# A decoder step of one layer: the search's counts shared between VectorE and ScalarE, rotary tables fetched at another time, more places for scores, and new costs in the planner

## The chip, the core and the metric

One core of a Trainium2 chip runs the whole step as one program. The metric is the device time in microseconds from launch to end; a profiled execution has besides it a span, from the first instruction to the last, which all views of the trace go by.

## The reference

One layer over 1024 prompt tokens and 64 sample tokens (8 requests of 8 tokens over a paged cache of 512), model width 1024. What matters here is the attention over selected keys:

```python
    dots = jnp.einsum('bthd,bld->bthl', qi.astype(jnp.float32), ki_all.astype(jnp.float32))
    score = jnp.einsum('bth,bthl->btl', wi.astype(jnp.float32), jax.nn.relu(dots)) * IDX_SCALE
    score = jnp.where(causal[None], score, -jnp.inf)
    _, idx = lax.top_k(score, n_sel)
```

Eight small indexer heads score every earlier token; the best 256 (130 for the samples) are kept, and the eight large heads attend over these alone. Around it stand a combined input projection with rotary turns of q, k and the indexer's q and k, a short convolution with gates, an output projection, a SwiGLU of width 2816, and a last gate with 256 extra features a token.

## The kernel before

**Tiling.** Activations are held feature by feature (128 partitions) times 1088 tokens, in chunks of 384, 384 and 320 tokens. Each fp32 factor is split in a high part (ScalarE copies it, rounded) and a low part (the rest, VectorE or GpSimd), and each product is three matmuls: high with high, high with low, low with high. So a projection of 128 features is 3 chunks of 24 matmuls each, and TensorE's total work is fixed by the shapes.

**The order of the work.** Nothing is scheduled by the compiler. A planner, the class Weaver, runs as the program is built. It has a clock for each engine, `T["pe"]`, `T["act"]`, `T["dve"]`, `T["pool"]`, and moves them with a cost for each operation (`act`, `tt`, `stt`, `ts`, `mm`, `mmf`, `mmg`, ...). Each stage is a generator that stops at `yield` for a buffer, an event or a moment; the planner goes on with the first side stream that is ready by these clocks, or else with the main stream, six matmuls at a time. The instructions come out in that order, and on the chip each engine runs its own in that order, waiting on semaphores. So a cost in the planner changes no instruction, only its neighbours. A side stream goes ahead if its data are there 0.2 us from TensorE's clock on and VectorE and ScalarE are planned no more than 5 us ahead (`LAG_E`, L292). A stream of the kind "dve" (the search) asks that VectorE's clock and its own time be within 1.5 us (L288).

```python
        self.go("act", 0.1 + n * 0.00084 + (1.3 if t != self.table else 0.0))
        c = max(0.426, n * 0.00168) if f32 else max(0.108, n * 0.000424)
        self.T["pe"] += max(0.108, n * 0.000424)
        self.T["pe"] += max(0.111, n * 0.000445 + 0.003)
```

These are the costs of a ScalarE operation (L127), of a side stream's matmul (`mm`, L181), of a projection's (`mmf`, L188) and of the second half's (`mmg`, L152).

**The stages.** Main: the indexer's k and q, then v, k, q, the convolution's gates, the branch gate ga; then, after everything else of the first half is done, output projection (two halves of 544 tokens), a projection of the extra features, gate-up by a seven-product scheme, down projection, last gate. Beside it as side streams, in this order of preference: `state_in`, `x_keep` (turns x to feature order and stores it in DRAM for the second half), `score_stream`, `samp_idx` (the samples' scores), `search` for the blocks 2 to 5 (group a) and for 6, 7 and the samples (group b), and at most three at a time of 32 `attn` streams (block, head pair) and 8 `samp_attn`. Attention starts when all scores are there (`ev_go`), and for blocks from 2 on when the block's threshold is known.

**Buffers.** Ring "p" has 5 places of 4 KB a partition: ki's high and low part hold two, `score_stream` two (query tiles, and `rbuf`, two places of 512 columns for rectified scores), so `x_keep` is left with one; later an attn stream takes two and a samp_attn three. Ring "L2" has 3: rotary tables take two, x_keep's turned tile one, later the convolution's rows. PSUM has three banks for projections ("pj"), two "at", two "pt", one "po". The planner doesn't know of the two places in `rbuf`; the chip's semaphores do.

**Rotary tables.** `load_tabs(64)` runs at the start, for the indexer's heads. `drop_tabs` (in `evac_qi`, last chunk of the last q block, and in `evac_q`) gives the two places back. The tables for k and q are fetched by `pre_tab(128)`, when the main stream comes to the first chunk of k.

**Scores and search.** For each head and each 512 columns `score_stream` does two matmuls into a bank "at", ScalarE rectifies into `rbuf`, and VectorE multiplies by the head's weight and adds to the scores (L139). `search` finds for each row the largest threshold that at least 256 scores reach, bit by bit of the float's 32: `cand` sets a bit, VectorE counts each block's scores from the threshold up (L1225, a compare with a summed output), `keep` compares the counts, `key` takes the bit. There are 33 rounds of counts: one for the sign, 31 bits, one last. What follows makes a bias of 0 or -2^100 for each score.

**Gate-up's start.** `norm` and four `factors` streams for each half p of the tokens make the sums and differences of the seven-product scheme (f_hi by ScalarE, f_lo by VectorE); weights go through the same treatment (`prep`, with `low` for the remainders). The first feature block runs on half 0, the second on half 0 and then 1.

## Time and profile before

| | |
|---|---|
| median of three runs | 1988.15 us (1983.81 to 1989.07) |
| the profiled execution: time, span | 1988.04 us, 1986.2 us |
| TensorE busy | 1942.3 us, 98% |
| VectorE, ScalarE, GpSimd busy | 1272.9 us (64%), 713.1 us (36%), 744.3 us (37%) |
| mean granted clock of TensorE | 0.989 of 2.4 GHz |

Times in rows are microseconds from the span's start unless marked ns. A line number is that of the helper that issues the operation, so groups are told apart by their tiles: pj, at, pt and po are PSUM banks, wh and wl (or whl) the parts of a weight tile, rt and ru the two halves of a rotary product, kidxT the samples' indexer keys, mx the row's maximum. Idle time of an engine is given with what ended it; where several semaphores were waited for, it is the last to come. A busy TensorE isn't one at full rate, so matmuls per stretch and the granted clock are read beside it.

### The profile page before, as it was taken

Reading aid. Unit: us, or ns where it says so; the run is one execution under the profiler, and the core shown is the slowest. Engines: PE = TensorE matmul, PEld = TensorE weight load, DVE = VectorE, ACT = ScalarE, POOL = GpSimd, SP = SyncE. Lnnn points to the kernel's source line nnn. Section 1 sums busy time; section 2 is a strip of 40 time slices with the busy share of each in tenths; the row PEclk is TensorE's granted clock in tenths of the full one; section 3 lists DMA queues with packets and bytes.
Section 4 is the critical chain, followed back from the end, with each engine's and each line's share of the span. In section 5 each row is a group of like instructions: output and inputs, shape, how many; then the busy total and the mean of one; then the engine's idle time right before and its main releaser. Section 6 shows DMA issues by size and latency. Waiting matters only on the chain.

```text
span 1986.2 us, 35764 instructions
## 1 busy us (share of the span) xinstructions
PE 1942.3 (98%) x13297; PEld 1863.8 (94%) x13297; DVE 1272.9 (64%) x2711; ACT 713.1 (36%) x1448; POOL 744.3 (37%) x661
## 2 busy tenths in 40 slices
PE   8998999999999999999999999999999999999998
PEld 5997879999999999879999999999999999999998
DVE  6534899899988896413437876566566653314754
ACT  5354433312433324433334532232232332213543
POOL 2533445323223233214454233232232364424883
PEclk9999999999999999999999999999999999999999
DMA  4574334222222222445443422222222353312343
GB/s 152 170 199 113 96 96 141 69 59 70 81 78 54 57 60 71 117 133 165 142 151 119 149 84 85 72 80 84 66 82 82 117 154 108 94 40 88 105 130 119
DMA packets 291240, 205.23 MB, mean 103 GB/s; under 512 B 28448, under 2 KB 270680, under 8 KB 291066
## 3 DMA queue, kind: packets, MB, share of 16 engines
q1 hardware_dynamic: 290742, 202.58, 34.4%
q8 instruction: 105, 1.72, 0.4%
q14 instruction: 69, 0.57, 0.1%
q10 hardware_dynamic: 324, 0.36, 0.1%
HBM read 151.43 MB, written 51.31 MB: 102 GB/s over the span
## 4 chain that ended last, share of the span: by engine, by line
PE 82%; DVE 4%; POOL 2%; issue 2%; DMA 1%; ACT 1%; SPq 0%; DVEq 0%; POOLq 0%; ACTq 0%
PE pj L154 44%; PE pj L190 27%; PE at L186 5%; PE po L186 4%; PE pt L197 3%; DVE scores L139 0%; DVE ru L135 0%; PE at L197 0%; POOL wl L150 0%; DVE junk L1225 0%; POOL rt L150 0%; POOL x L150 0%; DVE x L135 0%; DMA wraw<-in_w_down 0%; POOL x L2154 0%
## 5 line engine op out<-in xcount | busy, mean ns | idle before, releaser
L150 POOL TENSOR_TENSOR wl<-wraw,wh 128x512 fp32r<-128x512 f32 (+2 forms) x233 | 298.9, 1286 | 648.5 <-ACT wh L131 638.9
L190 PE MATMUL pj<-h_hi,wh 128*128 128x384 f32 (+2 forms) x1197 | 406.6, 340 | 0.3 <-ACT wh L131 0.3
L190 PE MATMUL pj<-h_hi,wl 128*128 128x384 f32 (+2 forms) x1197 | 393.7, 329 | 0.7 <-POOL wl L150 0.7
L190 PE MATMUL pj<-h_lo,wh 128*128 128x384 f32 (+2 forms) x1197 | 393.4, 329 | 0.0
L190 PEld LDWEIGHTS pj<-h_hi,wh 128*128 128x128 f32 (+1 forms) x1197 | 225.8, 189 | 16.4 <-issue 12.4
L131 ACT ACTIVATE wh<-wraw 128x512 fp32r<-128x512 f32 (+2 forms) x233 | 141.4, 610 | 277.5 <-PE pj L154 134.8
L190 PEld LDWEIGHTS pj<-h_lo,wh 128*128 128x128 f32 (+1 forms) x1197 | 226.1, 189 | 2.6
L190 PEld LDWEIGHTS pj<-h_hi,wl 128*128 128x128 f32 (+1 forms) x1197 | 225.5, 188 | 1.8 <-POOL wl L150 1.1
L154 PE MATMUL pj<-f_hi,whl 128*128 128x272 f32 x1056 | 208.3, 290 | 2.6 <-DVE whl L135 2.6
L154 PE MATMUL pj<-f_hi,wl 128*128 128x272 f32 x704 | 203.6, 289 | 0.5 <-DVE wl L135 0.5
L154 PE MATMUL pj<-f_hi,wh 128*128 128x272 f32 x704 | 203.4, 289 | 0.0
L154 PE MATMUL pj<-f_lo,wh 128*128 128x272 f32 x704 | 202.7, 288 | 0.0
L135 DVE TENSOR_TENSOR x<-pj,x 128x272 f32<-128x272 f32 (+2 forms) x144 | 67.0, 468 | 173.8 <-PE pj L154 170.6
L154 PE MATMUL pj<-m_hi,wh 128*128 128x272 f32 (+2 forms) x586 | 176.0, 300 | 0.9 <-ACT tha L131 0.5
L154 PE MATMUL pj<-m_hi,wl 128*128 128x272 f32 (+2 forms) x586 | 175.6, 300 | 0.0
L154 PE MATMUL pj<-m_lo,wh 128*128 128x272 f32 (+2 forms) x586 | 175.6, 300 | 0.0
L154 PEld LDWEIGHTS pj<-f_hi,whl 128*128 128x128 f32 x1056 | 170.5, 191 | 2.8 <-DVE whl L135 2.8
L154 PE MATMUL pj<-f_lo,whl 128*128 128x272 f32 x528 | 153.3, 290 | 0.0
L154 PEld LDWEIGHTS pj<-f_hi,wl 128*128 128x128 f32 x704 | 133.0, 189 | 0.8 <-DVE wl L135 0.8
L154 PEld LDWEIGHTS pj<-f_hi,wh 128*128 128x128 f32 x704 | 132.9, 189 | 0.0
L154 PEld LDWEIGHTS pj<-f_lo,wh 128*128 128x128 f32 x704 | 132.8, 189 | 0.0
L150 POOL TENSOR_TENSOR whl<-wraw,whl 128x512 fp32r<-128x512 f32 (+1 forms) x67 | 91.9, 1374 | 78.9 <-ACT whl L131 78.6
(367 smaller groups left out, 4534.1 us busy)
## 6 DMA issues: line engine op xcount, KB each, us to landing
wraw<-in_w_in SPq DMA_DIRECT2D x112, 256.0 KB
wraw<-in_w_gate_up SPq DMA_DIRECT2D x92, 256.0 KB
wraw<-in_w_down SPq DMA_DIRECT2D x40, 256.0 KB
wraw<-in_w_out SPq DMA_DIRECT2D x32, 256.0 KB
wraw<-in_w_ple_gate SPq DMA_DIRECT2D x32, 256.0 KB
x<-in_x_prompt SPq DMA_DIRECT2D x13, 512.0 KB
q_lo<-m_scr SPq DMA_DIRECT2D x19, 272.0 KB
m_scr<-q_lo SPq DMA_DIRECT2D x17, 272.0 KB
```

What stands on the lines that cost most here:

```text
L131: self.nc.scalar.activation(out, in_, func, **kw)
L135: self.nc.vector.tensor_tensor(out, a, b, op=op)
L150: self.nc.gpsimd.tensor_tensor(out, a, b, op=op)
L154: self.nc.tensor.matmul(ps, l, r, start=start, stop=stop)
L186: self.nc.tensor.matmul(ps, l, r, start=start, stop=stop)
L190: self.nc.tensor.matmul(ps, l, r, start=start, stop=stop)
L197: self.nc.tensor.transpose(ps, in_, ident)
```

## The change

The planner's costs of matmuls go from 0.424 to 0.45 ns a column and 1 ns (the second half's `mmg` is left as it is); the stream limits of 0.2 and 5 us become fields of a stream, and `norm` and `factors` of half 1 set theirs to 1.5 us. Ring "p" has 8 places; `rbuf` has four. The tables for k and q are fetched by a stream that starts where the indexer's tables are dropped, and the main stream waits for its event. In `search`, the blocks 4, 5, 6 and 7 are counted by ScalarE for the 31 bits: a sign of (threshold minus score) with summed output, which is the number below minus the number above. `keep` therefore compares with `lt` by "less or equal", and VectorE counts the other blocks from below. A score equal to the threshold counts half, so at the end the key's next larger value is tested once more with VectorE's exact counts and taken if it holds. The samples' attention is planned with longer times for page loads and GpSimd's scaling. No matmul is added or taken away.

```diff
-        c = max(0.426, n * 0.00168) if f32 else max(0.108, n * 0.000424)
+        c = max(0.426, n * 0.00172) / beside if f32 else max(0.11, n * 0.00045 + 0.001)
...
-        self.T["pe"] += max(0.108, n * 0.000424)
+        self.T["pe"] += max(0.11, n * 0.00045 + 0.001)
...
-                    ok = self._ready(s) <= pe + 0.2 and self.T["dve"] <= pe + LAG_E and self.T["act"] <= pe + LAG_E
+                    ok = self._ready(s) <= pe + s.ahead and self.T["dve"] <= pe + s.lag and self.T["act"] <= pe + s.lag
...
-    tp_ = tagged(tpool, "p", 5)
+    tp_ = tagged(tpool, "p", 8)
...
+    ev_tab = Ev()
+
+    def tabs_in(kind):
+        yield {"L2": 2}
+        load_tabs(kind)
+        ev_tab.t = W.move + 1.2
...
             if c == 2 and m == 3:
                 drop_tabs()
+                W.spawn(tabs_in(128))
...
-        rbuf = tp_([P, 2, 512], name="relu")
+        rbuf = [t[:, e] for t in (tp_([P, 2, 512], name="relu"), tp_([P, 2, 512], name="relu")) for e in range(2)]
...
-                    r = rbuf[:, used % 2]
+                    r = rbuf[used % 4]
...
+        def signs():
+
+            te, t0 = W.cur.t, W.cur.t
+            for i, q in enumerate(group):
+                if q in by_sign:
+                    m, L = lim(q)
+                    junk = tpool.tile([P, 1024], BF, tag="junk_s", name="junk_s", bufs=1)
+                    W.cur.t = t0
+                    W.go("act", 0.2)
+                    W.act(junk[:m, :L], score[q], AF.Sign, L, scale=-1.0, bias=cand[:m, i:i + 1].bitcast(F32),
+                          accum_out=cnt[:m, i:i + 1])
+                    te = max(te, W.cur.t)
+            W.cur.t = t0
+            return te
...
             W.stt(cand, key, 1 << b, msk, OP.bitwise_or, OP.bitwise_xor, G)
-            counts(OP.is_ge)
+            te = signs()
+            counts(OP.is_lt, on_dve)
+            W.cur.t = max(W.cur.t, te)
+            yield None
+            W.stt(keep, cnt, 1.0, lt, OP.mult, OP.is_le, G)
             W.stt(key, keep, b, key, OP.logical_shift_left, OP.bitwise_or, G)
             yield None
...
+        nc.vector.memset(cnt, 0.0)
+        counts(OP.is_ge, by_sign)
+        yield None
...
-        W.cur.t = t_k + 1.0
+        W.cur.t = t_k + 3.0
...
-        W.go("pool", 0.15 + LS * 0.00105)
+        W.go("pool", 0.15 + LS * 0.0029)
...
+        W.cur.lag = 5.0 if p == 0 else 1.5
...
-    sw = {64}
-
     def pre_tab(kind):
         def f(c):
-            if kind not in sw:
-                sw.add(kind)
-                yield {"L2": 2}
-                load_tabs(kind)
             if kind == 64:
                 yield ev_h[c]
                 if c == 0:
                     yield {"p": 2}
+            else:
+                yield ev_tab
         return f
...
-        W.spawn(search([2, 3, 4, 5], "a"), kind="dve", front=False)
-        W.spawn(search([6, 7, "s"], "b"), kind="dve", front=False)
+        W.spawn(search([2, 3, 4, 5], "a", (4, 5)), kind="dve", front=False)
+        W.spawn(search([6, 7, "s"], "b", (6, 7)), kind="dve", front=False)
```

## Rows read from the trace of the kernel before

**Rows 1.** The page's first part: busy time of each engine over the whole span, its share and its instructions.
```profile
PE 1942.3 (98%) x13297; PEld 1863.8 (94%) x13297; DVE 1272.9 (64%) x2711; ACT 713.1 (36%) x1448; POOL 744.3 (37%) x661
```

**Rows 2.** Windows of 50 us. Columns: the stretch and its length in us, then for each engine its busy us and (x) its instructions, the mean granted TensorE clock, the DMA engines' share and GB/s.
```profile
250.00:300.00 50.00, 46.81 (x250) 39.96 (x250) 46.06 (x88) 20.88 (x42) 23.36 (x20) 1.00 0.30 89
...
400.00:450.00 50.00, 50.00 (x304) 50.00 (x304) 46.58 (x123) 9.50 (x18) 11.14 (x12) 1.00 0.21 55
...
900.00:950.00 50.00, 50.00 (x304) 48.47 (x303) 16.71 (x24) 16.12 (x35) 20.15 (x17) 1.00 0.62 187
```

**Rows 3.** Windows of 10 us, with the same columns.
```profile
150.00:160.00 10.00, 6.95 (x25) 4.19 (x23) 3.47 (x7) 2.79 (x7) 3.01 (x3) 0.66 0.33 83
210.00:220.00 10.00, 10.00 (x48) 7.92 (x48) 8.07 (x22) 5.18 (x14) 3.29 (x3) 0.83 0.35 101
320.00:330.00 10.00, 7.28 (x34) 6.84 (x35) 9.53 (x26) 3.49 (x11) 8.13 (x12) 0.83 0.55 161
1130.00:1140.00 10.00, 7.27 (x41) 7.06 (x42) 9.90 (x17) 4.06 (x9) 4.24 (x3) 0.76 0.27 77
1140.00:1150.00 10.00, 10.00 (x74) 10.00 (x73) 9.16 (x17) 5.32 (x9) 3.00 (x2) 0.89 0.27 79
```

**Rows 4.** What TensorE waited for from 140 to 300 us: us in total, times, the longest.
```profile
PE at L186 <- ACT relu L131: 7.1, 4, 2.3
PE at L186 <- DVE kidxT L144: 4.0, 2, 3.1
```

**Rows 5.** The order of time from 138 to 162 us, VectorE and the SP queue (start, us, engine, line, operation, out<-in; in brackets the idle time before it and what the profile puts it down to), and the stores of x_keep in the whole run (ns: least, median, longest; first and last start).
```profile
143.37 0.64 SPq L163 DMA_DIRECT2D cos<-c_cos  x1
...
149.97 0.56 DVE L135 TENSOR_TENSOR rt<-pj,cos 128x384 f32<-128x384 f32 x1 [8.01 <-DMA out_new_v_prompt<-to]
...
L163 SPq DMA_DIRECT2D x_scr<-xT x9: 532/558/627, 79.2 to 207.6; - x9
```

**Rows 6.** The tile relu: the accumulation that reads it (ns: least, median, longest; first and last start), and what its engine waited for ahead of the instructions that touch it.
```profile
L139 DVE SCALAR_TENSOR_TENSOR scores<-relu,wi_c,scores x70: 341/750/1860, 106.7 to 301.3; 128x512 f32<-128x512 f32 x42, 128x384 f32<-128x384 f32 x14, 128x128 f32<-128x128 f32 x7, 128x256 f32<-128x256 f32 x7
...
  DVE scores L139: 23.3, 14
```

**Rows 7.** VectorE's groups by shape: the counts and the read of a count (busy us, mean ns), then when the counts of each of the two groups ran (first and last start).
```profile
L1225 DVE TENSOR_SCALAR_CACHE_REDUCE junk<-scores,candb 128x1024 uint8<-128x1024 f32 x33 | 42.2, 1279 | 1.2
...
L1225 DVE TENSOR_SCALAR_CACHE_REDUCE junk<-scores,candb 128x896 uint8<-128x896 f32 x33 | 37.8, 1146 | 1.2
...
L1225 DVE TENSOR_SCALAR_CACHE_REDUCE junk<-scores,canda 128x768 uint8<-128x768 f32 x33 | 33.4, 1012 | 1.2
L1225 DVE TENSOR_SCALAR_CACHE_REDUCE junk<-scores,canda 128x640 uint8<-128x640 f32 x33 | 29.0, 879 | 1.2
...
L1225 DVE DVE_READ_ACCUMULATOR junk<-scores,canda 128x1 f32 x132 | 10.9, 83 | 0.0
...
L1225 DVE TENSOR_SCALAR_CACHE_REDUCE junk<-scores,canda x132: 611/814/1016, 218.3 to 460.7; 128x384 uint8<-128x384 f32 x33, 128x512 uint8<-128x512 f32 x33, 128x640 uint8<-128x640 f32 x33, 128x768 uint8<-128x768 f32 x33
...
L1225 DVE TENSOR_SCALAR_CACHE_REDUCE junk<-scores,candb x66: 1145/1213/1281, 469.3 to 709.9; 128x896 uint8<-128x896 f32 x33, 128x1024 uint8<-128x1024 f32 x33
```

**Rows 8.** ScalarE's groups by shape: weight split, exponentials, the read of their sums, and the loads of function tables (busy us, mean ns, idle before).
```profile
L131 ACT ACTIVATE wh<-wraw 128x512 fp32r<-128x512 f32 x213 | 133.3, 628 | 193.4 <-PE pj L190 112.1 <-PE pj L154 58.3 <-issue 8.5
...
L131 ACT ACTIVATION_READ_ACCUMULATOR p<-p,mx 128x1 f32 x64 | 12.1, 188 | 0.0
...
L131 ACT ACTIVATE p<-p,mx 128x1024 f32<-128x1024 f32 x8 | 9.2, 1151 | 0.7 <-DVE mx L144 0.6
...
L131 ACT ACTIVATE p<-p,mx 128x896 f32<-128x896 f32 x8 | 8.3, 1039 | 4.4 <-DVE mx L144 4.4
...
L131 ACT ACTIVATE p<-p,mx 128x768 f32<-128x768 f32 x8 | 7.4, 930 | 2.2 <-DVE mx L144 2.2
...
L131 ACT ACTIVATE p<-p,mx 128x640 f32<-128x640 f32 x8 | 6.6, 822 | 0.8 <-DVE mx L144 0.8
...
L131 ACT ACT_TABLE_LOAD x4 | 5.1, 1283 | 3.2 <-issue 3.2
```

**Rows 9.** What TensorE waited for from 300 to 350 us (two of the lines).
```profile
PE pt L197 <- POOL p L1306: 1.5, 1, 1.5
PE po L186 <- DVE ptl L135: 1.5, 2, 1.2
```

**Rows 10.** What TensorE waited for from 720 to 1000 us (one of the lines).
```profile
PE pt L197 <- POOL psmp L1552: 1.5, 2, 1.2
```

**Rows 11.** What TensorE waited for from 1100 to 1160 us (one of the lines), and two of VectorE's instructions there.
```profile
PE pj L154 <- DVE whl L135: 2.6, 1, 2.6
...
1135.28 0.68 DVE L135 TENSOR_TENSOR whl<-wraw,whl 128x512 fp32r<-128x512 f32 x1
...
1150.96 0.43 DVE L135 TENSOR_TENSOR f_lo<-q_lo,f_hi 128x272 fp32r<-128x272 f32 x1
```

**Rows 12.** Windows over the searches, columns as in the second group.
```profile
301.00:461.00 160.00, 156.48 (x966) 154.90 (x965) 147.92 (x410) 44.67 (x105) 57.77 (x70) 0.99 0.33 90
461.00:712.00 251.00, 250.82 (x1614) 246.05 (x1613) 227.38 (x600) 87.06 (x185) 71.51 (x84) 1.00 0.24 65
```

**Rows 13.** ScalarE's groups from 360 to 740 us: exponentials and one tanh.
```profile
L131 ACT ACTIVATE p<-p,mx 128x384 f32<-128x384 f32 (+5 forms) x40 | 29.7, 743 | 13.3 <-DVE mx L144 13.1
...
L131 ACT ACTIVATE thb<-pj 128x384 f32<-128x384 f32 (+1 forms) x18 | 8.5, 474 | 42.0 <-PE pj L190 42.0
```

More of the change, by code (lines that the diff above doesn't have):

```diff
@@ L97, in __init__ @@
         self.front = self.queued = False
+        self.ahead, self.lag = 0.2, 5.0
 IDLE = "idle"
@@ L179, in later, with mm @@
         self.pending.append((self.cur.t, fn))
-    def mm(self, ps, l, r, n, start, stop, f32=False):
+    def mm(self, ps, l, r, n, start, stop, f32=False, beside=1):
         s = max(self.T["pe"], self.cur.t - 0.15)
-        c = max(0.426, n * 0.00168) if f32 else max(0.108, n * 0.000424)
+        c = max(0.426, n * 0.00172) / beside if f32 else max(0.11, n * 0.00045 + 0.001)
         self.T["pe"] = s + c
@@ L269, in run @@
         m = Stream(main)
-        LAG_D, LAG_E = 1.5, 5.0
+        LAG_D = 1.5
         while True:
@@ L1137, in score_stream @@
         tiles, seen, used = {}, [], 0
-        yield {"p": 2}
+        yield {"p": 3}
         qbuf = tp_([P, 2, 4, P], F32R, name="qstk")
-        rbuf = tp_([P, 2, 512], name="relu")
+        rbuf = [t[:, e] for t in (tp_([P, 2, 512], name="relu"), tp_([P, 2, 512], name="relu")) for e in range(2)]
         def fetch(w):
@@ L1197, in score_stream, with search, lim @@
                 W.cur.t = t0
-        W.give("p", 4)
+        W.give("p", 5)
         scores_done()
-    def search(group, nm):
+    def search(group, nm, by_sign):
         G = len(group)
+        def lim(q):
+            return (NS, LS) if q == "s" else (P, (q + 1) * P)
         for q in group:
@@ L1211, in search, with counts @@
         cnt = tpool.tile([P, G], F32, name=f"cnt{nm}")
+        lt = tpool.tile([P, G], F32, name=f"lt{nm}")
         for i, q in enumerate(group):
-            nc.vector.memset(N[:, i:i + 1], float(TOPK_S if q == "s" else TOPK))
+            n = float(TOPK_S if q == "s" else TOPK)
+            nc.vector.memset(N[:, i:i + 1], n)
+            nc.vector.memset(lt[:, i:i + 1], lim(q)[1] - 2 * n + 1 if q in by_sign else lim(q)[1] - n)
         nc.vector.memset(cand, 0)
         nc.vector.memset(cnt, 0.0)
-        def lim(q):
-            return (NS, LS) if q == "s" else (P, (q + 1) * P)
-        def counts(op):
+        def counts(op, which=None):
             for i, q in enumerate(group):
+                if which is not None and q not in which:
+                    continue
                 m, L = lim(q)
@@ L1226, in counts @@
                                         accum_out=cnt[:m, i:i + 1])
-            W.stt(keep, cnt, 1.0, N, OP.mult, OP.is_ge, G)
+        def signs():
[11 more added lines that the diff above has]
+            return te
+        on_dve = [q for q in group if q not in by_sign]
         counts(OP.is_ge)
+        W.stt(keep, cnt, 1.0, N, OP.mult, OP.is_ge, G)
         W.ts(key, keep, 31, None, OP.logical_shift_left, None, G)
@@ L1914, in norm @@
             room(p)
+        W.cur.lag = 5.0 if p == 0 else 1.5
         yield {"at": 2, "Q": 1}
```

18 lines of the change are left out of this document (added).

## The prediction

> **What bounds the kernel now.** I read the page's busy shares first: TensorE is busy for 1942.3 of 1986.2 us [rows 1]. The profiled execution took 1988.04 us, that is its span and 1.8 us around it, and agrees with the median of 1988.15, so sums made on the one hold for the other. In a kernel like this a busy engine off TensorE is worth nothing by itself; a change can only give back time in which TensorE stands still, or runs at its lower clock. So I looked next for that time. Where projections alone run, 50 us hold 304 matmuls [rows 2], 0.1645 us each for a mean of 362.7 columns (chunks of 384, 384 and 320); where search and projections run together (400 to 450 us) it holds 304 as well, with VectorE busy 46.58 of the 50 us. A VectorE at 93% thus costs TensorE nothing there. From 250 to 300 us it holds only 250. Then the 10 us windows with a low clock [rows 3]: at 150 to 160 the mean grant is 0.66, at 210 to 220 and 320 to 330 it is 0.83, at 1130 to 1140 0.76, at 1140 to 1150 0.89. Every one follows a wait of TensorE of over 2 us or two shorter ones close together, and since the lower level (1.2 GHz) is half of the upper (2.4 GHz), a mean of 0.66 over 10 us is 3.4 us lost on top of the wait. Then the waits themselves, stretch by stretch [rows 4, 9 to 11].
>
> The program is a list of instructions that a planner has put in order with its own cost for each. So I ask of each part: which wait goes, what the engine that is freed or loaded does then, and whether the planner's costs are as long as the rows.
>
> **Rotary tables early.** At 149.97 us VectorE starts the first rotary product of K after 8.01 us of idle [rows 5]. The bracket names an output transfer, the last of the queue to land before it; the tables it reads were issued just ahead, at 143.37 [rows 5]. The eight-column copy into kidxT that a TensorE matmul needs stands behind that product in VectorE's order, and TensorE waits for it: the longest of the two waits on kidxT is 3.1 us [rows 4], and the low clock after it costs 3.4 us [rows 3]. With the tables fetched when those of the indexer's rotary products are done, some 30 us sooner, both go: 6.5 us at most. The two issues move ahead of weight loads and of the reloads of x on SP's queue; if their places in L2 are not free, SP stands and later loads with it. The price is between nothing and the wait for a rope or two, of some three 0.56 us pieces each as at 149.97 [rows 5], 2 to 3 us, and the double-buffered weights cover it. x_keep is left with one L2 place instead of up to three; its stores ended at 207.6 us [rows 5] and nothing reads them before the second half, so a delay of tens of us is covered. I take 6.0 us of gain, ends 0 and 6.5.
>
> **Four places for rectified scores.** ScalarE's relu waits 23.3 us in 14 places for the VectorE accumulation that reads the place it wants [rows 6], and while it waits it doesn't empty PSUM: TensorE waits 7.1 us in four places, at most 2.3 us [rows 4]. The longest is the one ahead of the low clock at 210 us (1.7 us). Together 8.8 us. Two more places are worth two accumulations of 0.75 us [rows 6], 1.5 us of each wait. Of four waits of 1.8 us in the mean that takes 1.5 each, 6.0, and most likely the low clock, 1.7; against it, signs of about 1 us now stand in ScalarE's order between relus. I take 5.5 us, ends 0 and 8.8.
>
> **The counts on ScalarE.** VectorE loses, for each of 31 bits, the counts of 640 and 768 columns in the first group and of 896 and 1024 in the second: 0.879 + 1.012 + 1.146 + 1.279 us [rows 7] with 0.083 for each read, 4.65 us, 144 us in all. The exact last test puts back one such round (4.65 us) and some sixteen small operations on a few columns a group. ScalarE gains 31 rounds of four signs. No sign stands in the trace; the nearest rows are the exponentials with a pointer bias and an accumulated sum, 0.822, 0.930, 1.039 and 1.151 us and 0.188 for each read [rows 8]: 4.69 us a round, 145 us in all. So the work only changes engine. It was hidden: the two groups ran one after the other from 218 to 461 and from 469 to 712 us [rows 7], and TensorE lost almost nothing in 301 to 712 us but the few us of [rows 9] (156.48 of 160 and 250.82 of 251 us busy, [rows 12]). The searches will end sooner, perhaps by 100 to 200 us, attention follows sooner, and since projections are left to fill TensorE in any case, that is worth nothing in itself. What it can give is in places where attention waits for a loaded VectorE: the first heads wait 3.0 us between 300 and 350 us [rows 9] with 1.7 us of low clock; I take 2.0 of these 4.7 (from -2, if a sign stands ahead of an exponential). At the samples' attention, where the planner's waits for page loads and the pool's scaling are also made longer, the 1.5 us of waits on that scaling [rows 10] could go: I take 1.0, ends -1 and 1.5.
>
> **Gate-up's start.** The change lets the factors of the second half of the tokens be planned only while VectorE and ScalarE are less than 1.5 us ahead (5 before). The wait there, 2.6 us for whl [rows 11] with 2.4 and 1.1 us of low clock [rows 3], is a weight remainder that starts on VectorE only at 1135.28 because factors stand ahead of it. But VectorE is full there (9.90 and 9.16 of 10 us, [rows 3]) until the last remainder of those factors ends at 1151.4 [rows 11], and the first product with the second half needs them: if the weight comes sooner the factors come later, and TensorE waits a few us further on. I take 1.0, ends -3 and 6.1.
>
> **The planner's new costs.** A projection matmul was costed at 0.424 ns a column, 0.1538 us for 362.7 columns where 0.1645 is measured [rows 2]. The planner thus put 7% more TensorE work beside the other engines' work than it believed: a cushion. With 0.45 ns and 1 ns it has 0.1642, and the cushion is gone, while ScalarE's own costs stay short: a round of four signs is 4 x 0.2 + 4 x 0.1 + 3328 x 0.00084 = 4.00 us in its book and 4.69 by the rows, 0.69 x 31 = 21.4 us too little over the search. What queues behind a late sign is every relu, weight split and PSUM copy of ScalarE, and on VectorE, which stands at the keep operation until the signs have counted, every evacuation behind that. The planner has no slack against that but 1.5 us of lead for a search step, up to 5 us for the others, and the three projection banks of 24 matmuls (3.9 us each). New waits cost between 0 (ScalarE was busy 44.67 of 160 and 87.06 of 251 us [rows 12]; with 145 us of signs spread over 300 us it is at some 80%) and 27.4 us (below). I take 6.0, nearer to nothing, since in the DVE-bound stretch of [rows 2] work that was just as tight ended without loss, though it had the cushion.
>
> **Sum:** -6.0 - 5.5 - 2.0 - 1.0 - 1.0 + 6.0 = -9.5 us, on 1988.0: **1978.5 us**. The forecast's own range is 1966 to 1982.
>
> **Rivals.**
> *More comes off than that:* the upper ends of tables, places, heads, samples and gate-up (6.5 + 8.8 + 4.7 + 1.5 + 6.1 = 27.6 us) with 1 to 2 us of new waits: about 1962. For it: each of these waits has one cause, and the change names it. Against it: waits in a planned order mostly move. 0.08.
>
> *Nothing measurable:* new waits of 12 to 20 us on ScalarE's longer queue, each over 2 us with its 1.7 to 3.4 us of low clock, take back 15.5 us of gain: 1983 to 1994, middle 1988. For it: ScalarE's other work is costed short as well, such as the weight split of 512 columns, 0.628 us by the row [rows 8] and 0.53 in the planner's book. 0.20.
>
> *Slower, by ScalarE's drift:* place, 300 to 500 us, when both searches' signs run beside attention. ScalarE's deficit of 21.4 us and the lost cushion (7% of 200 us, 14 us) are 35.4 us; less some 8 us that lead and banks absorb, 27.4. With 15.5 gained: 2000 us. It decides from the point where ScalarE is planned nearly full, since a deficit drains in any gap: both groups' signs in turn, one pair of rounds each 5 to 6 us, would do that. 0.19.
>
> *Signs aren't in the loaded function table:* The trace has four table loads in all, of 1.283 us [rows 8], with relu, copy and exponential used side by side, and shows no sign. If each of the exponentials and tanhs beside the search (40 and 18 in 380 us [rows 13]) is switched to and back, that is 58 x 2 x 1.283 = 149 us of ScalarE time on 132 busy (at the rate of 87.06 in 251 us, [rows 12]) and 145 of signs: 426 us in a stretch of 380, and some 45 us are lost, 2033 us. The Trainium skill ("ScalarE: Activation LUTs", section "Table sets: the hidden batching unit") says that cheap functions, relu, copy, identity and abs, are in every set as filler, doesn't name sign among them, and prices a switch at 2.66 us, by which the same 116 switches would be 309 us. The trace agrees for relu and copy, which cause no load. 0.03.
>
> **How the numbers follow.** Forecast 0.50. About 0.3%, 6 us, is what a measurement of this kernel can tell from no change: faster is below 1982, slower above 1994. Forecast and first rival give faster 0.58, the second same 0.20, the last two slower 0.22. For 8 in 10 the range leaves out about 0.07 below and 0.11 above: 1962 to 1999.
>
> **What would show it.** Right: no 8 us idle of VectorE before the first rotary product of K, no wait on kidxT over 2 us, clock 1.00 at 150 to 160 us; relu's waits on the accumulation under 8 us; searches that overlap and end before 600 us; still four table loads. Gate-up's start should keep most of its loss, as a wait for factors or weights. Wrong: waits of TensorE on ScalarE or VectorE between 300 and 550 us over 10 us in sum, with clock below 0.95 there; or table loads by the dozen.

## The result and the profile after

The changed kernel takes 2014.25 us (2012.23 to 2019.87, four runs) where the kernel before, timed on the same chip, takes 1988.13: a ratio of 1.0143, 95% interval 1.0128 to 1.0158. It is slower by 26 us. The forecast was 1978.5 us, and the wider of its two ranges ended at 1999.

The page's first part and its row of the granted clock, after (the columns are those of [rows 1]; the clock in tenths, one digit for each fortieth of the span):
```profile
PE 1952.6 (97%) x13297; PEld 1867.2 (93%) x13297; DVE 1153.4 (57%) x2512; ACT 834.6 (41%) x1696; POOL 745.3 (37%) x661
...
PEclk9999989999999999999999989999999999999999
```
VectorE has lost 119.5 us of work and ScalarE has gained 121.5, as the change intends. TensorE has the same 13297 matmuls and takes 27.3 us more of span.

Where the time went is read from a count that needs no model: how many matmuls TensorE has done by a given time. Each number is the (x) of TensorE in a window that starts with the span.

| kernel | by 280 us | by 460 us | by 1100 us | by 1300 us |
|---|---|---|---|---|
| before | 1417 | 2487 | 6667 | 8207 |
| after | 1428 | 2363 | 6503 | 7992 |

At 280 us the changed kernel is 11 matmuls ahead. At 460 it is 124 behind; before does (2487 - 1417) / 180 = 5.94 a us there, so that is 21 us. At 1100 it is 164 behind, 25 us at the 6.53 a us of before from 460 to 1100, and at 1300 it is 215 behind, 28 us at 7.7 a us. (The mix of wide and narrow matmuls differs a little between kernels, so such a figure is good to a few us.) From 11 ahead to 215 behind is 226 matmuls: 135 are lost from 280 to 460 us, 40 from 460 to 1100, and 51, some 7 us, from 1100 to 1300, at gate-up's start. So most of the loss arises between 280 and 460 us.

Windows of after (columns of [rows 2]); the first two are stretches of [rows 3], the last is the stretch of the loss:
```profile
150.00:160.00 10.00, 10.00 (x61) 8.87 (x61) 4.57 (x9) 6.08 (x15) 1.77 (x2) 1.00 0.49 132
210.00:220.00 10.00, 9.06 (x48) 6.48 (x47) 9.71 (x19) 7.36 (x17) 3.95 (x4) 1.00 0.32 95
248.00:258.00 10.00, 9.08 (x32) 7.42 (x33) 6.74 (x17) 5.08 (x13) 1.90 (x3) 0.66 0.11 32
289.00:299.00 10.00, 7.60 (x36) 7.60 (x37) 7.53 (x29) 5.89 (x16) 2.73 (x3) 0.66 0.18 60
...
410.00:420.00 10.00, 6.27 (x24) 6.18 (x24) 8.81 (x26) 6.57 (x16) 4.03 (x4) 0.66 0.25 67
...
1170.00:1180.00 10.00, 3.66 (x13) 3.03 (x14) 8.58 (x18) 3.54 (x7) 0.40 (x1) 0.50 0.08 29
280.00:460.00 180.00, 158.73 (x937) 153.21 (x937) 158.33 (x481) 122.82 (x274) 72.89 (x91) 0.95 0.33 93
```
The two low clocks of [rows 3] at 150 and 210 us are gone (1.00, and 61 matmuls where 25 stood). New ones stand at 248, 289 and 410 us, at 0.66, and at 1170 us with 0.50: there TensorE ran the whole 10 us at the lower level. From 280 to 460 us it is busy for 158.73 of 180 us (before: 175.46, with clock 0.99). VectorE is busy for 158.33 there and ScalarE for 122.82: neither is full.

What TensorE waits for, after: first from 140 to 300 us (compare [rows 4]; the 5.3 us of mx are the same wait as in the second view), then from 280 to 460, then from 1120 to 1200 us (compare [rows 11]).
```profile
PE at L187 <- DVE mx L1352: 5.3, 1, 5.3
PE at L187 <- ACT relu L132: 4.4, 4, 2.2
PE at L187 <- ACT kidxT L132: 1.5, 1, 1.5
```
```profile
PE at L187 <- DVE mx L1352: 6.5, 2, 5.3
PE po L187 <- DVE ptl L136: 5.9, 4, 3.7
PE at L187 <- DMA qh<-qh_scr: 5.7, 4, 3.7
PE pt L198 <- POOL p L1364: 2.8, 3, 1.4
```
```profile
PE pj L155 <- DVE f_lo L136: 6.5, 3, 4.4
PE pj L155 <- ACT f_hi L132: 2.0, 1, 2.0
```
From 280 to 460 us it is mostly VectorE that TensorE waits for, in attention (the row maxima mx and the split ptl: 12.4 of 20.9 us). The next is the load of a head's queries, qh (5.7 us, 0.5 before); the longest of these loads was held for 3.7 us until VectorE's lob, the last step of group a's search, gave back a place of the same ring. ScalarE has no row there. At gate-up the wait for the weight remainder of [rows 11] is gone, and waits for the factors of the second half of the tokens stand in its place.

ScalarE's groups by shape, after: the signs with the idle time ahead of them, the read of their counts, the table loads. Under them the tile junk_s: what VectorE waited for from it (us, times).
```profile
L132 ACT ACTIVATE junk_s<-scores,candb 128x1024 bf16<-128x1024 f32 x31 | 35.6, 1150 | 1.0
L132 ACT ACTIVATE junk_s<-scores,candb 128x896 bf16<-128x896 f32 x31 | 32.2, 1039 | 19.3 <-DVE candb L140 19.0
L132 ACT ACTIVATE junk_s<-scores,canda 128x768 bf16<-128x768 f32 x31 | 29.0, 936 | 1.0
L132 ACT ACTIVATE junk_s<-scores,canda 128x640 bf16<-128x640 f32 x31 | 25.6, 826 | 41.9 <-DVE canda L140 41.9
...
L132 ACT ACTIVATION_READ_ACCUMULATOR junk_s<-scores,candb 128x1 f32 x62 | 11.6, 188 | 0.0
...
L132 ACT ACT_TABLE_LOAD x4 | 5.1, 1283 | 3.2 <-issue 3.2
```
```profile
  DVE keepb L140: 19.9, 16
  DVE keepa L140: 3.9, 7
```
The signs take what the exponentials of [rows 8] take, to 6 ns, and there are still four table loads. ScalarE stands idle for 41.9 and 19.0 us ahead of its signs until VectorE's candidate comes, and VectorE stands for 23.8 us until signs have counted (10.0 of them from 280 to 460 us): in a chain of rounds each waits for the other. That VectorE is the later one is read from what TensorE waits for, above, and from the lengths that follow.

VectorE's small steps of group a, after (four columns, mean ns), and one stretch in order of time, VectorE and GpSimd (columns of [rows 5]):
```profile
L140 DVE SCALAR_TENSOR_TENSOR keya<-keepa,keya 128x4 int32<-128x4 int32 x31 | 12.0, 388 | 1.1
L140 DVE SCALAR_TENSOR_TENSOR keepa<-cnta,lta 128x4 int32<-128x4 f32 x31 | 11.9, 382 | 4.1 <-ACT junk_s L132 3.9
L140 DVE SCALAR_TENSOR_TENSOR canda<-keya,mska 128x4 int32<-128x4 int32 x31 | 11.8, 381 | 0.8
```
```profile
298.36 0.17 DVE L140 SCALAR_TENSOR_TENSOR canda<-keya,mska 128x4 int32<-128x4 int32 x1
...
301.21 1.30 POOL L151 TENSOR_TENSOR wl<-wraw,wh 128x512 fp32r<-128x512 f32 x1 [3.33 <-ACT wh L132]
301.79 0.73 DVE L140 SCALAR_TENSOR_TENSOR keepa<-cnta,lta 128x4 int32<-128x4 f32 x1
302.46 1.01 POOL L151 TENSOR_TENSOR rt<-rt,ru 128x384 f32<-128x384 f32 x1
302.56 0.93 DVE L140 SCALAR_TENSOR_TENSOR keya<-keepa,keya 128x4 int32<-128x4 int32 x1
303.43 1.28 POOL L151 TENSOR_TENSOR wl<-wraw,wh 128x512 fp32r<-128x512 f32 x1
303.52 1.21 DVE L140 SCALAR_TENSOR_TENSOR canda<-keya,mska 128x4 int32<-128x4 int32 x1
304.69 1.41 POOL L1364 TENSOR_SCALAR p<-p,mx 128x128 f32<-128x128 f32 x4
```
The same step on four columns takes 0.17 us while GpSimd is idle and 1.21 us while GpSimd works. Read the ends: keepa ends at 302.52 and GpSimd's wl at 302.51; keya at 303.49 and rt at 303.47; canda at 304.73 and wl at 304.71. Three times a step of a few columns ends 10 to 20 ns after the GpSimd instruction that was running when it started. The planner books 0.134 us for each. These three are not picked out: of the 190 such steps of both searches in this trace, the 134 beside an idle GpSimd took 144 to 166 ns, and the 38 that took more than 250 ns all started beside a running GpSimd instruction and ended 7 to 27 ns after the end of one.

What stood ahead of the longest of TensorE's waits, the 5.3 us on mx (VectorE first, the last line is TensorE's):
```profile
280.14 1.24 DVE L140 SCALAR_TENSOR_TENSOR keepa<-cnta,lta 128x4 int32<-128x4 f32 x1
281.42 0.93 DVE L140 SCALAR_TENSOR_TENSOR keya<-keepa,keya 128x4 int32<-128x4 int32 x1
282.27 1.83 DVE L140 SCALAR_TENSOR_TENSOR scores<-relu,wi_c,scores 128x512 f32<-128x512 f32 x1
284.14 0.99 DVE L136 TENSOR_TENSOR scores<-scores,b 128x128 f32<-128x128 f32 x1
...
291.04 0.29 DVE L1352 CUSTOM_DVE_ANT_0 p<-at,b 128x128 f32<-128x128 f32 x1
291.40 0.47 PE L187 MATMUL at<-k_hi,qh 128*128 128x128 f32 x1 [5.26 <-DVE mx L1352]
```
The two small steps take 1.9 us more than they are booked for, the accumulation 1.2 (0.66 booked) and the addition 0.8 (0.23 booked); a little later VectorE stands 0.66 us until a sign has counted. So in this wait the small steps are the largest part, but not the only one.

### The profile page after: what moved, and what is told of

Read it like the earlier page. It is cut to its first block, busy times and chain, and to the rows that moved or that the text cites. A ratio compares the mean times of both kernels' runs of the same rounds, so it can differ in the third digit from the quotient of the medians.

```text
span 2013.5 us, 35917 instructions
## 1 busy us (share of the span) xinstructions
PE 1952.6 (97%) x13297; PEld 1867.2 (93%) x13297; DVE 1153.4 (57%) x2512; ACT 834.6 (41%) x1696; POOL 745.3 (37%) x661
## 4 chain that ended last, share of the span: by engine, by line
PE 72%; DVE 6%; issue 2%; ACT 2%; POOL 1%; DMA 1%; SPq 0%; DVEq 0%; POOLq 0%; ACTq 0%
PE pj L155 43%; PE pj L191 20%; PE po L187 4%; PE at L187 3%; PE pt L198 2%; DVE junk L1239 1%; ACT junk_s L132 1%; DVE cum L1319 0%; POOL wl L151 0%; DMA q<-ple_scr 0%; DVE q_lo L136 0%; DVE x L136 0%; POOL whl L151 0%; DVE f_lo L136 0%; DVE cv L140 0%
## 5 line engine op out<-in xcount | busy, mean ns | idle before, releaser
L151 POOL TENSOR_TENSOR rt<-rt,ru 128x384 fp32r<-128x384 f32 (+5 forms) x81 | 82.4, 1026 | 105.1 <-ACT ru L132 52.5
```

The source lines that it names most:

```text
L151: self.nc.gpsimd.tensor_tensor(out, a, b, op=op)
```

## The experiments

The theory at this point: VectorE is late against the planner's book between 200 and 520 us, because the book has its two-input operations too short, and the old, too short cost of a matmul had hidden that. The rivals: ScalarE's queue of signs is late (the forecast's own rival); the larger ring lets attention heads start into a loaded VectorE; the small steps are simply many. In the expectations theory A is the lost cushion of 7%, theory B the two searches beside attention on VectorE, theory C the larger ring. Ratios are to the kernel before on the same chip, with their 95% intervals. The runs are from several chips, on which the kernel before takes 1985.9 to 1988.4 us, so a difference between two runs' times is good to some 2 us.

**The old matmul costs in the changed kernel.**
```diff
-        c = max(0.426, n * 0.00172) / beside if f32 else max(0.11, n * 0.00045 + 0.001)
+        c = max(0.426, n * 0.00168) / beside if f32 else max(0.108, n * 0.000424)
...
-        self.T["pe"] += max(0.11, n * 0.00045 + 0.001)
+        self.T["pe"] += max(0.108, n * 0.000424)
```


> The changed kernel with the planner's old costs of a matmul (0.424 ns a column in mm and mmf), all else as changed. Theory A (the 7% cushion): most of the new waits between 280 and 460 us go, about 2014 - 17 = 1997 us. Theory B (the searches with signs run beside rotary products and attention on VectorE): the waits stay, 2006 us or more. Theory C (three attention streams at a time by the larger ring): as B.


1997.63 us, 1.0056 [1.0039, 1.0073]: 16.6 us come back from two cost lines that add no work and remove none, as theory A had it. By 1100 us 6620 matmuls are done (after: 6503).

**All counts on VectorE in the changed kernel**, the rest as it is:
```diff
-        W.spawn(search([2, 3, 4, 5], "a", (4, 5)), kind="dve", front=False)
+        W.spawn(search([2, 3, 4, 5], "a", ()), kind="dve", front=False)
```
and the same for group b.


> The changed kernel with every block counted by VectorE for the 31 bits, none by ScalarE (the last test then counts nothing), all else as changed. Theory B: the searches run one after the other again, attention of the blocks from 2 on starts after 450 us, and the waits between 280 and 460 us fall from 24 us to under 8: about 1996 us. Theory A: VectorE is as full as before and without the cushion, so 2008 us or more. Theory C: some waits go since attention comes later, 2002 to 2008 us.


1997.06 us, 1.0053 [1.0038, 1.0069]: 17.2 us come back here too. By its expectation that is theory B's result, and theory A's (2008 us or more) is missed: without the cushion, but with all counts on VectorE, this stretch loses nothing. Windows over the loss for these two kernels, in this order:
```profile
280.00:460.00 180.00, 165.68 (x984) 162.99 (x983) 154.43 (x455) 118.24 (x264) 71.36 (x83) 0.95 0.31 85
```
```profile
280.00:460.00 180.00, 178.17 (x1106) 176.64 (x1104) 171.74 (x473) 46.63 (x107) 70.01 (x81) 1.00 0.33 93
```
With VectorE *fuller* by 13 us (171.74 for 158.33), TensorE loses nothing in this stretch. So it isn't VectorE's load as such that hurts. One reading is that it is how far the book is from it: counts are booked as long as they are, small steps aren't, and with the counts on VectorE the 93 small steps of group a spread over 238 us (207.6 to 445.8) instead of 175, with 4 of group b's steps ahead of 460 us instead of 50. But the small steps still take 11.9 us more than booked between 280 and 460 us here (19.2 after, 12.8 before), without a cushion and without loss, so the distance to the book isn't the whole account: that attention meets one search there and not two is as good a reading of this run.

**The old lead of 5 us for gate-up's factors**, in the changed kernel:
```diff
-        W.cur.lag = 5.0 if p == 0 else 1.5
+        W.cur.lag = 5.0
```


> The changed kernel with the lag of norm and factors of the second half of the tokens at 5 us again. All theories of the first half: nothing moves ahead of 1000 us. If the lag is what makes TensorE wait for f_lo and f_hi at gate-up's start (8.5 us of waits and 6.8 us of low clock there): 5 to 8 us less than the changed kernel, about 2007 us, with the wait for a weight back in its place. If VectorE is simply too full there: within 2 us of 2014.


2008.52 us, 1.0098 [1.0071, 1.0126]: 5.7 us come back by the medians. The f_lo and f_hi waits go, and the wait for whl of [rows 11] returns. The 20 us after 1160 us, first after, then with this edit:
```profile
1160.00:1180.00 20.00, 11.48 (x74) 10.42 (x73) 17.98 (x39) 9.06 (x16) 1.68 (x2) 0.75 0.17 55
```
```profile
1160.00:1180.00 20.00, 18.24 (x144) 17.88 (x143) 17.64 (x32) 9.54 (x18) 5.64 (x4) 1.00 0.24 74
```

**A smaller ring**, in the changed kernel (6 places for p, one of them not given back to attention):
```diff
-    tp_ = tagged(tpool, "p", 8)
+    tp_ = tagged(tpool, "p", 6)
...
-        W.give("p", 5)
+        W.give("p", 4)
```


> The changed kernel with a ring p of 6 places of which one isn't given back after the scores, so that x_keep has one place and attention five (two streams at a time) as before the change; rectified scores keep their four places. Theory C: the waits of attention between 280 and 460 us fall by half, about 2002 us. Theories A and B: 2010 us or more.


2026.42 us, 1.019 [1.0162, 1.0219]: slower by another 12 us. The rival of the ring (theory C, 2002 us) falls; with fewer places the waits on VectorE are longer (ptl 10.7 us in nine places, where after has 6.2 in five).

**The parts alone, on the kernel before.** First the tables, the four places with the ring, and the samples' times together; then the new matmul costs alone; then the new search alone.


> The kernel before with the rotary tables early, the larger ring with four places for rectified scores, and the longer planned times in the samples' attention; matmul costs, lag and search as before the change. Each of costs and search, undone alone, took 17 us off the changed kernel. If the two add (two separate troubles): 2014 - 17 - 17 - 6 (lag) = 1974 us, some 13 us faster than before. If they are one trouble that needs both (VectorE late in a stretch without slack): undoing the second gains little more, 1985 to 1992 us.


1986.76 us, 1.0005 [0.9992, 1.0018]: no change. The parts do what they say: by 280 us 1481 matmuls are done, 64 more than before, some 11 us. By 460 us the lead is 32, by 1100 us 9. Half of it is given back from 280 to 460 us, to waits for ptl (4.4 us), mx (3.2) and GpSimd's p (2.6) that were 1.5, nothing and 1.5 before; most likely attention, coming earlier, meets more of the search on VectorE.

> The kernel before with the planner's new matmul costs alone. Theory A (the cushion): without it the loaded VectorE reaches TensorE also without signs, 1994 to 2002 us. If the cushion only counts beside the signs: within 4 us of 1987.


2006.93 us, 1.0098 [1.0076, 1.0121]: 19 us lost by telling the planner the truth about TensorE alone. About half is lost ahead of 280 us (1345 matmuls by then, 72 fewer than before, some 14 us), where TensorE waits 14.0 us on relu in eight places; by 1100 us 153 are missing. Ahead of 280 us it is above all the accumulations of scores that are booked too short.

> The kernel before with the new search alone (signs, last test, and the added stop between counting and keeping, by which the two searches run side by side). Theory B: attention meets both searches on VectorE, 1996 to 2004 us. If the signs only hurt without the cushion: within 4 us of 1987.


2002.16 us, 1.0079 [1.0057, 1.0101]: 16 us lost by the new search alone, with TensorE waiting for ptl (6.6 us) and mx (3.8).

**One search after the other**, in the kernel before with the new search: group b starts when a is done.
```diff
+        if nm == "b":
+            yield ev_first
...
+        if nm == "a":
+            ev_first.t = W.cur.t
```


> The kernel before with the new search alone (it took 16 us more than before), and the second group's search held until the first has its thresholds. If two searches side by side, with three small VectorE operations each a bit, crowd VectorE as attention runs: back to 1986 to 1991 us. If it is the signs in ScalarE's queue and VectorE's stand at keep: 1998 us or more.


1997.88 us, 1.0045 [1.0031, 1.0059]. Side by side costs at most some 4 us of the 16: the two intervals overlap, and the control below shows that a new order alone moves the time by 3. The rest comes with one search at a time as well. The expectation had put 1998 us down to the signs in ScalarE's queue and VectorE's stand at keep, so this run speaks for that rather than for two searches that crowd VectorE.

**Tables alone and places alone**, on the kernel before.


> The kernel before with the rotary tables for k and q fetched early, alone. As predicted before the change: 6 us less, 1980 us, with VectorE's 8 us idle at 145 us, the 3 us wait on kidxT and the low clock after it gone. If the wait only moves: within 2 us of 1986, with as much lost ahead of 300 us.


1989.49 us, 1.002 [1.0007, 1.0032].


> The kernel before with the ring p of 8 and four places for rectified scores, alone. As predicted: 5.5 us less, 1980.5 us, TensorE's 7 us of waits on relu down to 2 to 3 us. Rival: the late VectorE, no longer held back at relu, is met a little later by the first attention heads: the loss goes from ahead of 300 us to 300 to 350 us, and the time stays at 1986.


1988.78 us, 1.0026 [1.0013, 1.004]. Each removes the waits that it aims at and gains nothing: without VectorE's idle time ahead of K's rotary products, TensorE waits 7.0 us on relu in seven places and once 4.3 us on ptl; without the relu waits, 3.7 us on mx and 4.7 on kidxT.

**How much any other order moves the time.** In the kernel before, one cost of the planner is made 1 ns longer (VectorE's two-tensor operations).
```diff
-        self.go("dve", 0.1 + n * 0.00104)
+        self.go("dve", 0.101 + n * 0.00104)
```


> A control: the kernel before with 1 ns more on the planner's cost of each two-tensor operation of VectorE. Nothing is meant by it; the orders of the engines come out somewhat otherwise. It tells how far any new planning moves the time: within 2 us of 1986 if single effects of 3 to 5 us may be read as causes, 4 us or more off if they may not.


1992.92 us, 1.0017 [1.0003, 1.003]. A second one, 10 ns on ScalarE's operations, gave the like:


> A second control: the kernel before with 10 ns more on the planner's cost of each ScalarE operation. As the first control: within 2 us of 1986, or 4 us and more off it, if any new order moves the time that far.


1990.98 us, 1.0014 [1.0002, 1.0026]. So a new order as such can cost 3 us; the tables' and places' 1.002 and 1.0026 are hardly more. That an order can gain as much by luck wasn't seen, but two controls don't rule it out.

**VectorE's lengths in the planner's book**, in the changed kernel: 0.28 us more for each score accumulation, 1.0 us more for the small steps of each bit. No instruction is added. The 0.28 is what the trace shows in the mean (the 70 accumulations take 58.6 us where 39.9 are booked); the 1.0 is more than it shows (0.75 in group a, 0.24 in group b), and 0.7 of it stands at keep, where VectorE also waits for the signs.
```diff
+                    W.go("dve", 0.28)
...
+            W.go("dve", 0.3)
...
+            W.go("dve", 0.7)
```


> The changed kernel with the planner told how long VectorE's operations were measured to be in the score stretch: 0.28 us more for each accumulation of scores, and 1.0 us more for the three small operations of a bit (they took 0.39 to 0.55 us each beside scores, 0.13 planned). No instruction changes. If TensorE waits because VectorE's real queue is longer than the planned one: the waits between 280 and 460 us fall from 34 to about 18 us, near 1997 us. If the planned lengths don't matter: 2010 us or more.


1994.97 us, 1.0046 [1.0034, 1.0058]: 19.3 us come back. By 280 us 1482 matmuls are done, 54 more than after, and from 280 to 460 us 1052, 20 fewer than before instead of 135; by 1100 us 6669 are done, as before (6667). What is left stands at gate-up (8165 by 1300 us, before 8207: 5.5 us). The lead of 5 us on top of that:


> The changed kernel with the lag at 5 us again and the planner told of VectorE's measured lengths (as in the run that took 19 us off). If the two parts add: 1995 - 6 = 1989 us, and what stays over the kernel before is attention beside two searches. If they don't: 1993 us or more.


1988.35 us, 0.9996 [0.9985, 1.0008]. The two together take back the whole 26 us.

**The same book with the old search.** First with the old matmul costs (tables, places, samples' times, book), then with the new ones, which is all of the change but the search and gate-up's lead.


> Tables early, larger ring with four places, longer planned times of the samples' attention; search, lag and matmul costs as before the change; and the planner told of VectorE's measured lengths (0.28 us more for each accumulation of scores, 1.0 us more for the small operations of a bit). If VectorE's late queue is what the first attention heads meet: 8 to 12 us less than without these lengths, 1974 to 1979 us, faster than both kernels. If not: 1984 to 1988 us.


2034.9 us, 1.0249 [1.0231, 1.0267]. A miss: 49 us above the kernel before. With TensorE booked 7% too short and VectorE at its full length the plan most likely paces the search too slowly: group b's counts end at 777 us (712 before). TensorE waits 27.2 us on m_hi in four places ahead of the out-projection and once 11.1 us for a head's qh.


> As the one before, with the new matmul costs. With VectorE's lengths in the planner's book the cushion isn't needed: within 4 us of the one before, 1974 to 1982 us. If the cushion covers more than these operations: 1990 us or more.


1983.23 us, 0.9986 [0.9975, 0.9996]: between its two expectations, and the one version that beats the kernel before, by 0.14%, which is no more than the controls moved the time. From 280 to 460 us TensorE is busy for 179.53 of 180 us.

**Shorter GpSimd instructions**, to tell whether the small steps are long because of GpSimd. Two-input operations of 256 columns or more go in pieces of 128, with the planner's costs left alone.
```diff
+        if len(out.shape) == 2 and n >= 256:
+            for x in range(0, n, 128):
+                y = min(n, x + 128)
+                self.nc.gpsimd.tensor_tensor(out[:, x:y], a[:, x:y], b[:, x:y], op=op)
+            return
```


> The changed kernel with GpSimd's two-input multiplications and additions of 256 columns or more written as pieces of 128 columns each; the planner's costs, and so what it books, are left as they are. Theory V (VectorE runs late because its operations with two inputs in SBUF stand still until GpSimd's running operation has ended, so that a 4-column step of the search that takes 134 to 166 ns beside an idle GpSimd takes 600 to 1290 ns beside a busy one): the longest of these steps fall to some 400 ns, VectorE gains some 15 us between 200 and 520 us, and the time falls from 2014 to 1998 to 2006. Theory N (VectorE is late by the number of its operations alone, 62 pairs of steps more than before, and the long steps are waits for other things that the trace puts into their durations): the long steps stay long, and the time stays at 2010 or above, a little more by the added GpSimd instructions.


2028.41 us, 1.0214 [1.0194, 1.0235]. Theory V's time is missed; by its time alone the run would fall to theory N (2010 us or above, though by more than a little), but the long steps shorten, which N excludes. The trace says why. Group a's small steps in it, then GpSimd's largest group, after (512 columns) and here (128):
```profile
L140 DVE SCALAR_TENSOR_TENSOR keepa<-cnta,lta 128x4 int32<-128x4 f32 x31 | 10.8, 349 | 3.8 <-ACT junk_s L132 3.6
L140 DVE SCALAR_TENSOR_TENSOR keya<-keepa,keya 128x4 int32<-128x4 int32 x31 | 9.6, 310 | 1.1
...
L140 DVE SCALAR_TENSOR_TENSOR canda<-keya,mska 128x4 int32<-128x4 int32 x31 | 8.6, 276 | 0.8
```
```profile
L151 POOL TENSOR_TENSOR wl<-wraw,wh 128x512 fp32r<-128x512 f32 x213 | 283.6, 1334 | 596.1 <-ACT wh L132 570.7 <-PE pj L191 5.9 <-DVE mx L145 4.5
```
```profile
L154 POOL TENSOR_TENSOR wl<-wraw,wh 128x128 fp32r<-128x128 f32 x892 | 433.0, 518 | 559.5 <-ACT wh L132 546.3 <-DVE mx L145 4.1 <-DVE ptl L136 1.9
```
The small steps shorten (1151 to 935 ns for the three; canda's longest from 1289 to 494 ns, but keepa's grows from 1244 to 1802), VectorE's busy time over the span falls from 1153.4 to 1090.4 us, and by 1100 us 6599 matmuls are done, 96 more than after: 15 us, the gain that theory V expected by that time, of which the small steps' 31 x 0.216 = 6.7 us are a part. But four pieces take 2.07 us where one took 1.33, GpSimd's work grows from 745.3 to 1018.7 us, and late in the kernel, where TensorE waits on GpSimd's chain (x 8.5 us, longest 7.0), more than that is lost.


> The kernel before with the early tables, the four places and larger ring, the samples' times, the new matmul costs and VectorE's measured lengths in the planner's costs (1983.2 without this edit), and with GpSimd's two-input operations of 256 columns or more in pieces of 128. The old search stays. Theory V: its small steps between counts shorten in the same way, and since the planner books them at their long lengths here, the gain is at most 2 to 4 us: 1979 to 1983. Theory N: 1983 to 1988, by the added instructions of GpSimd.


2016.32 us, 1.0157 [1.0143, 1.0171], 28 us above both expectations. With the longer book there is nothing to win back from VectorE (6622 matmuls by 1100 us, where the run without pieces has 6678), and the loss at the end remains.

## Why the prediction was wrong

**The step that failed first is "The planner's new costs", +6.0 us.** Alone, on the kernel before, the new matmul costs lose 19 us; in the changed kernel, undoing them brings back 16.6. The step saw that the cushion of 7% would go and looked for a queue that is booked too short; it found ScalarE's signs, 21.4 us, and took 6.0, nearer to nothing. It did not ask the same of VectorE. The numbers were in the trace of before: the small steps of group a took 0.413, 0.340 and 0.165 us (canda, keepa, keya) where 0.134 is booked for each, (0.918 - 0.402) x 31 = 16 us in the 232 us of that search, and the 70 accumulations of scores ahead of it took 58.2 us where 39.9 are booked. In the changed kernel it is (1.151 - 0.402) x 31 = 23 us in 175 us for group a, with group b's 31 x (0.634 - 0.399) = 7 us beside its end, and no cushion.

**The second is in "The counts on ScalarE": "worth nothing in itself", -2.0 us.** The new search alone, on the kernel before, loses 16 us, and undoing it in the changed kernel brings back 17.2. Costs and search don't add: 19 and 16 alone, 26 in all with gate-up's loss, and either one undone leaves 9 to 11 us, of which gate-up's lead is 5.7.

**What the runs show in their place** is that VectorE's work is planned too short beside a TensorE that is planned as it runs. More planned VectorE time in the changed kernel brings back 19.3 us, and with gate-up's lead restored all 26. It does so without signs too: with the old search and the new matmul costs the kernel takes 1983.2 us with the longer book, where the new costs without it take 2006.9 (the tables, places and samples' times by which the two differ besides change nothing alone); and the longer book with the old matmul costs ends at 2034.9. Which operations carry it isn't separated: the book was lengthened for accumulations and small steps together, and for the latter by more than they take. The trace favours the small steps in the stretch of the loss (19.2 us over the book from 280 to 460 us, where only one accumulation is left) and the accumulations ahead of it (17.8 us by 280 us).

**Why the steps are long** is shown by the trace more than by a run. The long ones start beside a running GpSimd operation and end when one ends, all 38 of them; with shorter GpSimd operations they shorten. The Trainium skill ("SBUF — State Buffer", section "SBUF: two separate sides") states the mechanism: VectorE and GpSimd share a pair of ports as an exclusive lock, and where a VectorE operation with two inputs in SBUF meets a GpSimd instruction that reads SBUF, the one that starts first holds the pair for its whole length and the other waits. The trace agrees, by ends 7 to 27 ns apart. The prediction costed the sixteen small operations and the rounds without asking what runs on GpSimd beside them. What part of the loss goes through the port, and what through the mere number of rounds in less time, stays open: the split that shortens GpSimd's hold also makes GpSimd slower.

**The rival "Slower, by ScalarE's drift"** had the lost cushion and the sign of the result right, and the place nearly. Of its mechanism part stays open. ScalarE's queue of relus and splits made TensorE wait nowhere from 280 to 460 us, and the engine that TensorE waited for was VectorE; but VectorE stood there for 10.0 us until signs had counted, the path that the prediction named, and no run books the signs alone at their length. By its own terms the sign of "wrong" did not come: from 300 to 550 us TensorE waits 7.4 us on VectorE and ScalarE, not over 10, with a clock of 0.98, not below 0.95. The longest wait, 5.3 us, ends at 291 us, ahead of that stretch.

**"Rotary tables early" (-6.0) and "Four places" (-5.5)**: mechanism right, worth wrong. The wait of TensorE for VectorE's copy into kidxT is gone (a 1.5 us wait for ScalarE's is left); the clock at 150 and 210 us is 1.00. With the tables alone VectorE's first rotary product starts at 142.12 us (149.97 before); in the changed kernel it starts at 147.94, after 10.46 us of idle time, but now waits for TensorE's own projection. ScalarE's relu waits 1.5 us on the accumulation where it waited 23.3 [rows 6]. The two and the samples' times put TensorE 11 us ahead by 280 us, and 32 of those 64 matmuls are lost again by 460 us, nearly all by 1100. The prediction asked what the engine that is freed does then, and for these two parts answered with full gains.

**"Gate-up's start" (-1.0)**: wrong in sign. The text itself said that the factors would come later if the weight comes sooner, and named -3 as the worst end; it costs 5.7 us: 8.5 us of waits for factors with 10 us at the lower clock, where 2.6 us of waits with 2.4 and 1.1 us of low clock had been.

**"The counts on ScalarE", what was right**: the sign is as long as the exponential (826, 936, 1039 and 1150 ns, reads 187 and 188), the searches overlap and end at 520 us, and the table loads stay four, so the last rival falls. The sum of 4.69 us a round was too long: a read starts some 0.09 us before its sign ends, and signs and reads together keep ScalarE busy for 134.0 us, 4.32 a round. **The samples' part** (-1.0) was never run by itself; the 1.5 us of waits on the scaling has no row any more, and a worth of that size can't be told from the noise of a new order.

## What to carry to other kernels

In an order made by a cost model, the error of one engine's costs can cover another's, so that correcting one alone costs time: compare every engine's costs with the trace, and the small operations above all, which here were wrong by the largest factor. Before giving VectorE more small two-input steps, look at what GpSimd runs beside them. And a wait that is removed may come back further on, as both did here; a run of the part alone shows it.

## What was not expected of the hardware

A VectorE step with two inputs in SBUF on 4 columns takes 0.14 to 0.17 us alone and up to 1.29 us beside a GpSimd operation; counts with one input and a summed output (512 columns, 746 ns before and after) and products out of PSUM (384 columns, 556 ns) don't lengthen. Not every step with one input is free of it: the compare that writes eq took 1.29 us on 8 columns beside GpSimd, where the one that writes lob took 0.22 on the same 8 beside an idle one. A sign with a pointer bias and an accumulated sum takes the time of an exponential of the same width and needs no table load of its own (four in the span, as before). GpSimd's subtractions cost 1334 ns for 512 columns and 518 ns for 128: a piece of a quarter is not a quarter of the time.
